# A two-layer hybrid trunk in split fp32: gate and up products as one 512-wide and one 256-wide matmul instead of three 256-wide

## The chip, the cores and the metric

The kernel runs on one core of a Trainium2 chip. The metric is the device time of one execution in microseconds (us). Engines are named as in the profile: PE (TensorE; PEld is its weight load), DVE (VectorE), ACT (ScalarE), POOL (GpSimd), SP (SyncE, which issues the loads).

## What is computed

256 tokens of width 1024 pass through two layers. Each layer is a half-step SwiGLU feed-forward, a mixing part (sparse attention in 8 heads beside a gated linear recurrence in 4), and a second half-step feed-forward:

```python
def swiglu(x, w_gate, w_up, w_down):
    return (jax.nn.silu(x @ w_gate) * (x @ w_up)) @ w_down

for l in range(DEPTH):                                   # 2
    x = x + 0.5 * swiglu(rmsnorm(x, ffn1_norm[l]), ffn1_w_gate[l], ffn1_w_up[l], ffn1_w_down[l])
    h = rmsnorm(x, mix_norm[l])
    proj = h @ w_in[l]
    ...
    x = x + jnp.concatenate([o_nsa, o_hg], axis=-1) @ w_out[l]
    x = x + 0.5 * swiglu(rmsnorm(x, ffn2_norm[l]), ffn2_w_gate[l], ffn2_w_up[l], ffn2_w_down[l])
```

The gate and up weights are 1024 x 2816, the down weights 2816 x 1024, all in fp32. So there are four feed-forwards in a run.

## The kernel before

**Split products.** A product W x in fp32 is made of three matmuls in the type fp32r: W's high part with x's high part, W's high part with x's low part, and W's low part with x's high part. The names `hi` and `lo` are the parts of a unit of weights, `xh` and `xl` those of the normed activations (transposed: 128 rows of the width by 256 tokens, 8 such tiles), `th` and `tl` those of the hidden activations.

**The stream of weights.** Weights come in units of 512 KB (1024 columns by 128 partitions) through SP into one of three `raw` buffers. ACT copies a unit to `hi` (L313), DVE, in the mixing part POOL also, subtracts it to `lo` (L326, L328); five split units are held (`RING`). A unit's place comes free when the matmuls have used it.

**Two ways of multiplying.** In `stream` (L463 to L465) 128 tokens of one half h are the stationary operand and 512 columns of weights move; the result of half h goes to an accumulator of `acc0` for h = 0 and of `acc1` for h = 1. In `wide_unit` (L493 to L495) 128 columns of weights are the stationary operand and all 256 tokens move; a block of 256 columns is [128, 2, 256], one PSUM bank. `acc0` and `acc1` have two slots each, each slot a tile of its own of one bank.

**A feed-forward.** First a block of 256 gate and 256 up columns goes through `stream`, one for each half (`both_done` at its end; in the very first feed-forward it uses activations that still lack the norm's factor, `rs`). Then ten times a gate block through `wide_unit` in `acc0` and an up block in `acc1`, each of two units with 2 x 4 steps (c, t). When a gate block ends, ACT reads it with Silu into a buffer `sg`; when an up block ends, DVE multiplies it by that `sg`; ACT copies the result to `th`, DVE subtracts to `tl`. Then the down product goes through `stream`, two blocks of 512 columns for each half, and DVE adds each to the residual (`resid`, L653). The mixing part's w_in and w_out products go through `stream` too, except the 512 columns each of `hf` and `hq` of the recurrence, which go through `wide_unit`.

**The order.** The order of instructions is not written down but made by a planner while the program is built: `Sched.run` holds generators as tasks, and at each step emits the op that could start first by modelled costs, plus a penalty by kind of task. An op with several engines to choose from (a copy, a subtraction) goes to the one that would end it first. Each engine then runs its instructions in that order, and waits for others by semaphores, which the tile framework sets from who wrote and read which tile.

Of the kernel before, what the change touches and what calls it, by code (L numbers as in the profile page):

```python
# [25 lines left out]
LARGE = 85.0   # the exponential of more could overflow  # L26
LEVELS = [0, 1, 2, 4, 8, 16, 32]

# columns of the constant array
# [9 lines left out]
# moving layout of the keys of a group: sel 1 | sel 0 | win 0 | win 1 | compressed  # L39
# [5 lines left out]
RING = 5       # split weight units held  # L45
RAW = 3        # unsplit weight units held
BOOT = 3       # units split by K tiles at the start
# when the rest of the inputs is loaded: after which unit of weights, half, from and to which 256 columns
BOOT_X = ((-1, 0, 1, 2), (0, 0, 2, 4), (2, 1, 0, 2), (3, 1, 2, 4))
FIRST = (-0.3, -0.4, 0.5, 1.3, 0.1, 0.6, 0.9, 0.2)  # L50
LAG = 4        # units by which the halves of the tokens are apart at a phase's ends
NBUF = 14      # general buffers of the mixing part
# [3 lines left out]
# how eager the tasks are (less: earlier)  # L56
# [43 lines left out]
class Op:  # L100
    """An instruction (or a few for one engine), with the engines that could run it, each with what it costs there."""
# [15 lines left out]
LOAD = 1.28    # a switch of ScalarE's tables  # L117
# [4 lines left out]
class Sched:  # L122
    """Emits the instructions of tasks that run side by side, in the order in which they could start.

    A task is a generator. It yields an Op (and is sent the op's end), or a request: wait for a key
    or a condition, set a key, acquire a slot (sent the slot), release it. An op waits for what its
    task has waited for or done before."""
# [26 lines left out]
    def resolve(self, t):  # L154
        """A request that isn't an op; whether it could be met."""
# [37 lines left out]
    def run(self):  # L193
        while self.tasks:
# [29 lines left out]
            if eng == "DMA":  # L224
                # its issue, then the transfer, which others hold up
                issued = end - cost + 0.475
                self.moved = max(issued + 0.65, self.moved) + cost
                end = self.moved + 0.87
# [7 lines left out]
def four(t):  # L236
    """Two K tiles of 512 columns as four of 256."""
    return t.rearrange("p a (b n) -> p (a b) n", b=2)
# [29 lines left out]
class Block:  # L268
    """Columns of a product that share an accumulator: [128 tokens, n] for each half, or, where the weights are the
    stationary operand, [128 columns, 2, 256 tokens]."""  # L270

    def __init__(self, n, done, wide=None):
        self.n, self.done, self.wide, self.ps = n, done, wide, {}


class Unit:
    """1024 x 128 of a block's weights: two K tiles of 512 columns, or four of 256."""
# [6 lines left out]
class Trunk(Sched):  # L284
    def __init__(self, ctx, tc, io, out):
# [5 lines left out]
        bank = lambda n: psum.tile([128, 512], F32, name=n)  # L291
        for h in range(2):
            self.slots[f"acc{h}"] = [(bank(f"acc{h}{i}"), []) for i in range(2)]
# [24 lines left out]
    def copy(self, out, in_, after=None):  # L318
        """A copy, by either of two engines."""
# [36 lines left out]
    def transposes(self, pairs):  # L356
        """pairs: (out, in)."""
# [9 lines left out]
    def rope_norm(self, st, n):  # L367
        """st [128, 2, n]: sums of squares in, inverse norms out, both in the first row."""
        yield self.ts(st[:, 1], st[:, 0], 1.0 / n[1], EPS, op0=OP.mult, op1=OP.add)
        yield self.rsqrt(st[:, 0], st[:, 1])  # L370

# [107 lines left out]
    def wide_unit(self, i, u, p):  # L479
# [4 lines left out]
        if u.first:  # L484
            (k.ps[0],) = yield acq(f"acc{k.wide}")
        ps = k.ps[0].rearrange("p (c t) -> p c t", c=2)
        hi, lo = (four(x) for x in self.split_w[i])
        f = self.nc.tensor.matmul

# [7 lines left out]
        def two(c, t):  # L497
            mm(c, t)
            mm(c, t + 1)

        for c in range(2):
            for t in (0, 2):
                yield self.P(6 * (0.0025 + 256 / 2400), lambda: two(c, t))
# [21 lines left out]
    def control(self):  # L525
        """One phase's memory after the other's."""
# [8 lines left out]
    def start(self):  # L535
        nc, per = self.nc, self.per
        self.X, self.XN, self.ss, self.rs = [], [], [], []
        self.XH, self.XL = (per.tile([128, 8, 256], F32R, name=n) for n in ("xh", "xl"))
# [22 lines left out]
    def pad(self):  # L561
        """Zeros that stay, of what only in part takes data."""
# [10 lines left out]
    def boot(self):  # L573
        """What the start waits for, in the order in which it is needed."""
# [34 lines left out]
    def first_turn(self, h, n):  # L609
        """The first product starts before the norm is known: of the inputs times the gains, transposed."""  # L610
# [47 lines left out]
    def norm(self, h, i):  # L658
        """The i-th norm of the half h: its transposed, split activations."""
# [32 lines left out]
    def ffn(self, l, pre):  # L692
# [27 lines left out]

        def wide_gate_done(b):
            def done(ps):
                yield wait(("open", p))
                (sg,) = yield acq("sg")
                yield self.A(sg, ps, AF.Silu)
                yield rel("acc0", ps)
# [4 lines left out]
        def wide_up_done(b):  # L731
            def done(ps):
                yield wait(("wg", p, b))
                sg = st["wg", b]
                yield self.tt(sg, ps, sg, OP.mult)
                yield rel("acc1", ps)
# [12 lines left out]
        for c in range(10):  # L749
            for a, (w, d) in enumerate(((wg, wide_gate_done), (wu, wide_up_done))):  # L750
                b = Block(512, d(c), wide=a)
# [27 lines left out]
        def opened(pool, p):  # L779
            self.slots["sg"] = [(pool.tile([128, 512], F32, name=f"sg{i}"), []) for i in range(4)]  # L780
# [58 lines left out]
    def mix(self, l):  # L839
# [69 lines left out]
        def values(h, br, src):  # L909
            """src [128, g, 64] -> split, between columns of zeros."""  # L910
# [171 lines left out]
        def attend_task(h, g):  # L1082
# [3 lines left out]
            # the heads' segments: branch, where in the scores, width, mask  # L1086
# [443 lines left out]
```

## Time and profile before

| | us |
|---|---|
| median of three runs | 1146.16 |
| the runs | 1146.1, 1149.26, 1146.16 |
| span of the profiled execution | 1147.0 |
| PE busy in it | 1080.8 (94%) |
| DVE busy | 720.7 (63%) |
| ACT busy | 571.7 (50%) |
| POOL busy | 200.5 (17%) |
| DMA, mean | 162 GB/s |

The profile is of one execution, and its span is 0.84 us above the median. The durations below are from it. An engine that is idle waits for what stands behind the arrow in its row. In rows of PE the time from one start to the next says what a matmul costs in a stream; the duration printed includes its passage through the array and overlaps the next one.

### The profile page before, as it was taken

How to read it: one execution, taken by the hardware profiler on the slowest of the kernel's cores; microseconds unless marked ns; L12 is line 12 of the kernel's file. 1: busy time of each engine (PE TensorE's matmuls, PEld its weight loads, DVE VectorE, ACT ScalarE, POOL GpSimd, SP SyncE). 2: the span in 40 equal slices, each digit the busy share in tenths (PEclk: the TensorE clock that was granted, in tenths of full speed). 3: DMA queues.
4: the chain of work that ended last, by engine and by line, in shares of the span. 5: the costliest groups of instructions: out<-in, count | busy, mean ns of one | idle time of the engine just before them, and what ended most of it. 6: DMA issues, size and time to landing. Idle time of an engine off the chain costs nothing.

```text
span 1147.0 us, 18786 instructions
## 1 busy us (share of the span) xinstructions
PE 1080.8 (94%) x7420; PEld 974.6 (85%) x7420; DVE 720.7 (63%) x1187; ACT 571.7 (50%) x899; POOL 200.5 (17%) x193
## 2 busy tenths in 40 slices
PE   5999999988879999999999999999898799999998
PEld 4999988777668799998879999877876688999986
DVE  5565544777998665554465555447889976655543
ACT  5554444465756554444354444434675555444432
POOL 2200000353554200000020000013635622000000
PEclk9999999998989999999999999999998899999999
DMA  7666655564313476666666666555551235766553
GB/s 220 197 188 194 188 185 185 148 167 129 110 55 93 147 200 187 184 185 184 188 171 199 187 178 190 181 161 160 144 167 56 74 110 145 204 184 183 183 157 121
DMA packets 154168, 186.16 MB, mean 162 GB/s; under 512 B 7568, under 2 KB 117984, under 8 KB 154080
## 3 DMA queue, kind: packets, MB, share of 16 engines
q1 hardware_dynamic: 154080, 184.96, 54.7%
q8 instruction: 58, 0.95, 0.3%
q14 instruction: 30, 0.25, 0.1%
HBM read 183.89 MB, written 1.05 MB: 161 GB/s over the span
## 4 chain that ended last, share of the span: by engine, by line
PE 75%; DVE 16%; issue 4%; DMA 2%; ACT 1%; POOL 1%; SPq 1%; DVEq 0%; POOLq 0%; ACTq 0%
PE acc L493 14%; PE acc L494 14%; PE acc L495 14%; PE acc L463 9%; PE acc L465 9%; PE acc L464 9%; DVE buf L326 2%; PE short L360 2%; DVE lo L326 2%; DVE xn L668 1%; DVE buf L1156 1%; DVE hx L326 1%; DVE kk L336 1%; DVE P L326 1%; DVE ptl L326 1%
## 5 line engine op out<-in xcount | busy, mean ns | idle before, releaser
L326 DVE TENSOR_TENSOR lo<-raw,hi 128x1024 fp32r<-128x1024 f32 (+2 forms) x302 | 365.6, 1214 | 286.5 <-ACT hi L313 285.5
L313 ACT ACTIVATE hi<-raw 128x1024 fp32r<-128x1024 f32 (+2 forms) x337 | 350.6, 1043 | 309.2 <-PE acc L465 110.8
L493 PE MATMUL acc<-xh,hi 128*128 128x256 f32 x1408 | 402.4, 286 | 0.0
L494 PE MATMUL acc<-xl,hi 128*128 128x256 f32 x1408 | 401.1, 285 | 0.0
L495 PE MATMUL acc<-xh,lo 128*128 128x256 f32 x1408 | 400.9, 285 | 0.0
L493 PEld LDWEIGHTS acc<-xh,hi 128*128 128x128 f32 x1408 | 273.2, 194 | 0.2
L494 PEld LDWEIGHTS acc<-xl,hi 128*128 128x128 f32 x1408 | 273.1, 194 | 0.1
L495 PEld LDWEIGHTS acc<-xh,lo 128*128 128x128 f32 x1408 | 273.0, 194 | 0.0
L463 PE MATMUL acc<-hi,th 128*128 128x512 f32 x352 | 139.5, 396 | 0.0
L464 PE MATMUL acc<-lo,th 128*128 128x512 f32 x352 | 139.2, 395 | 0.0
L465 PE MATMUL acc<-hi,tl 128*128 128x512 f32 x352 | 139.1, 395 | 0.0
L354 POOL TENSOR_TENSOR rs<-rs,half 128x1 f32<-128x1 f32 x12 | 7.0, 587 | 552.2 <-DVE rs L661 552.2
L328 POOL TENSOR_TENSOR lo<-raw,hi 128x1024 fp32r<-128x1024 f32 (+1 forms) x37 | 89.4, 2422 | 68.6 <-ACT hi L313 43.2
L463 PE MATMUL acc<-hi,xh 128*128 128x512 f32 (+1 forms) x240 | 98.6, 411 | 0.0
L465 PE MATMUL acc<-hi,xl 128*128 128x512 f32 (+1 forms) x240 | 93.0, 387 | 0.0
L464 PE MATMUL acc<-lo,xh 128*128 128x512 f32 (+1 forms) x240 | 92.7, 386 | 0.0
L465 PEld LDWEIGHTS acc<-hi,tl 128*128 128x128 f32 x352 | 66.1, 188 | 16.1
L463 PEld LDWEIGHTS acc<-hi,th 128*128 128x128 f32 x352 | 66.2, 188 | 15.6
L464 PEld LDWEIGHTS acc<-lo,th 128*128 128x128 f32 x352 | 66.1, 188 | 15.6
L313 ACT ACTIVATE sg<-acc 128x512 f32<-128x512 f32 (+1 forms) x46 | 26.1, 568 | 66.8 <-PE acc L495 64.4
L465 PEld LDWEIGHTS acc<-hi,xl 128*128 128x128 f32 x240 | 46.2, 193 | 9.3
L463 PEld LDWEIGHTS acc<-hi,xh 128*128 128x128 f32 x240 | 46.8, 195 | 6.8
(233 smaller groups left out, 1174.9 us busy)
## 6 DMA issues: line engine op xcount, KB each, us to landing
raw<-in_ffn_w_down_dram SPq DMA_DIRECT2D x88, 512.0 KB, 4.0
raw<-in_ffn_w_gate_dram SPq DMA_DIRECT2D x80, 512.0 KB, 3.8
raw<-in_ffn_w_up_dram SPq DMA_DIRECT2D x80, 512.0 KB, 4.1
raw<-in_w_in_dram SPq DMA_DIRECT2D x48, 512.0 KB, 3.7
raw<-in_w_out_dram SPq DMA_DIRECT2D x16, 512.0 KB, 3.8
buf<-in_cmp_w_dram SPq DMA_DIRECT2D x16, 256.0 KB, 5.1
raw<-in_ffn_w_gate_dram SPq DMA_DIRECT2D x13, 256.0 KB, 2.8
raw<-in_ffn_w_up_dram SPq DMA_DIRECT2D x13, 256.0 KB, 3.1
```

The source lines that it names most:

```text
L313: return ("ACT", c, lambda: self.nc.scalar.activation(out, in_, func, **k), TABLES.get(func))
L326: alts = [("DVE", 0.065 + 0.00104 * n, lambda: self.nc.vector.tensor_tensor(out, a, b, op), None)]
L328: alts.append(("POOL", 0.13 + 0.00213 * n, lambda: self.nc.gpsimd.tensor_tensor(out, a, b, op), None))
L336: lambda: self.nc.vector.tensor_scalar(out, a, s1, s2, **k), None)]
L360: self.nc.tensor.transpose(o, i, self.ident[:i.shape[0], :i.shape[0]])
L463: f(ps[:, :k.n], ah, hi[:, t, :k.n], start=st, stop=False)
L464: f(ps[:, :k.n], ah, lo[:, t, :k.n], start=False, stop=False)
L465: f(ps[:, :k.n], al, hi[:, t, :k.n], start=False, stop=sp)
L493: f(ps[:, c], hi[:, t, j], xh, start=u.first and c == t == 0, stop=False)
L494: f(ps[:, c], hi[:, t, j], xl, start=False, stop=False)
L495: f(ps[:, c], lo[:, t, j], xh, start=False, stop=u.last and c == 1 and t == 3)
L668: toks.append((yield self.V(576, lambda: nc.vector.scalar_tensor_tensor(self.XN[h][:, c], self.X[h][:, c], rs[:, 0:1], self.gains[0][:, c] ...
```

## The change

The two slots of `acc0` become the two halves (one bank each) of one tile `pair[0]` of [128, 2, 512], and so those of `acc1` in `pair[1]`. `xh` and `xl` become the halves of one tile `xx`, so that for each of the 8 K tiles the 256 columns of the high part and the 256 of the low part lie side by side. A gate or up block is now "paired": it takes both slots of its accumulator. A step (c, t) is one 512-wide matmul of the weights' high part with both parts of the activations (L500, into bank c), and one 256-wide of the weights' low part with the high part (L501, into the first half of the same bank). At a block's end `both_parts` adds the two halves: ACT copies the second halves of the two banks into an `sg` buffer, DVE adds the first halves. A gate block's Silu then runs from `sg` to `sg`; an up block takes an `sg` buffer of its own, for which there are now five, and the multiply reads two of them. The planner's cost of a group of steps changes with the number of matmuls. `hf` and `hq` keep three matmuls. Comments and docstrings, which the new file has not, are left out here.

```diff
-    def __init__(self, n, done, wide=None):
-        self.n, self.done, self.wide, self.ps = n, done, wide, {}
+    def __init__(self, n, done, wide=None, paired=False):
+        self.n, self.done, self.wide, self.paired, self.ps = n, done, wide, paired, {}
...
         bank = lambda n: psum.tile([128, 512], F32, name=n)
+        self.pair = []
         for h in range(2):
-            self.slots[f"acc{h}"] = [(bank(f"acc{h}{i}"), []) for i in range(2)]
+            t = psum.tile([128, 2, 512], F32, name=f"acc{h}")
+            self.pair.append(t)
+            self.slots[f"acc{h}"] = [(t[:, i], []) for i in range(2)]
         self.slots["short"] = [(bank(f"short{i}"), []) for i in range(3)]
         self.slots["po"] = [(bank("po"), [])]
         big = lambda n, dt: self.per.tile([128, 2, 512], dt, name=n)
...
             yield wait(u.need(h))
         k = u.block
         if u.first:
-            (k.ps[0],) = yield acq(f"acc{k.wide}")
-        ps = k.ps[0].rearrange("p (c t) -> p c t", c=2)
+            if k.paired:
+                k.ps[0] = yield acq(f"acc{k.wide}", 2)
+            else:
+                (k.ps[0],) = yield acq(f"acc{k.wide}")
+        ps = k.ps[0] if k.paired else k.ps[0].rearrange("p (c t) -> p c t", c=2)
         hi, lo = (four(x) for x in self.split_w[i])
         f = self.nc.tensor.matmul
+        def mm2(c, t):
+            j = slice(128 * c, 128 * c + 128)
+            x = self.XX[:, u.kt + t].rearrange("p a t -> p (a t)")
+            f(self.pair[k.wide][:, c], hi[:, t, j], x, start=u.first and t == 0, stop=False)
+            f(self.pair[k.wide][:, c, :256], lo[:, t, j], x[:, :256], start=False, stop=u.last and t == 3)
 
         def mm(c, t):
             j = slice(128 * c, 128 * c + 128)
...
             f(ps[:, c], lo[:, t, j], xh, start=False, stop=u.last and c == 1 and t == 3)
 
         def two(c, t):
-            mm(c, t)
-            mm(c, t + 1)
+            for x in (t, t + 1):
+                mm2(c, x) if k.paired else mm(c, x)
 
         for c in range(2):
             for t in (0, 2):
-                yield self.P(6 * (0.0025 + 256 / 2400), lambda: two(c, t))
+                yield self.P((4 if k.paired else 6) * 0.0133 + 0.64, lambda: two(c, t))
         yield rel("ring", self.split_w.pop(i))
         yield put(("wide", i))
         if u.last:
...
-        self.XH, self.XL = (per.tile([128, 8, 256], F32R, name=n) for n in ("xh", "xl"))
+        self.XX = per.tile([128, 8, 2, 256], F32R, name="xx")
+        self.XH, self.XL = self.XX[:, :, 0], self.XX[:, :, 1]
...
 
+        def both_parts(x, a):
+            x, t = x.rearrange("p (c t) -> p c t", c=2), self.pair[a]
+            yield self.A(x, t[:, :, 256:])
+            yield self.tt(x, t[:, :, :256], x, OP.add)
         def wide_gate_done(b):
             def done(ps):
                 yield wait(("open", p))
                 (sg,) = yield acq("sg")
-                yield self.A(sg, ps, AF.Silu)
-                yield rel("acc0", ps)
+                yield from both_parts(sg, 0)
+                yield rel("acc0", *ps)
+                yield self.A(sg, sg, AF.Silu)
                 st["wg", b] = sg
                 yield put(("wg", p, b))
             return done
 
         def wide_up_done(b):
             def done(ps):
+                (up,) = yield acq("sg")
+                yield from both_parts(up, 1)
+                yield rel("acc1", *ps)
                 yield wait(("wg", p, b))
                 sg = st["wg", b]
-                yield self.tt(sg, ps, sg, OP.mult)
-                yield rel("acc1", ps)
+                yield self.tt(sg, up, sg, OP.mult)
+                yield rel("sg", up)
                 s = slice(2 + 2 * b, 4 + 2 * b)
                 yield from self.split(st["th"][:, s], st["tl"][:, s], sg.rearrange("p (c t) -> p c t", c=2))
                 yield rel("sg", sg)
...
-                b = Block(512, d(c), wide=a)
+                b = Block(512, d(c), wide=a, paired=True)
...
-            self.slots["sg"] = [(pool.tile([128, 512], F32, name=f"sg{i}"), []) for i in range(4)]
+            self.slots["sg"] = [(pool.tile([128, 512], F32, name=f"sg{i}"), []) for i in range(5)]
```

The number of matmuls falls from 7420 by 1280. In the rows that follow, a name's number tells buffers apart: before, `acc00_63` and `acc01_64` are the two banks of `acc0`, `acc10_65` and `acc11_66` those of `acc1`; now `acc0_63` and `acc1_64` are the two tiles of two banks.

PE at the start of the first gate block of the first feed-forward. Before:

```order
L360 MATMUL short1_68<-ident_94,xn1_91 128x128 [waits DVE_49]
L360 MATMUL short1_68<-ident_94,xn1_91 128x128 x3
L493 MATMUL acc01_64<-xh_84,hi4_82 128x256 [waits Activation_49]
L494 MATMUL acc01_64<-xl_85,hi4_82 128x256 [waits DVE_49]
L495 MATMUL acc01_64<-xh_84,lo4_83 128x256
```

Now:

```order
L364 MATMUL short1_66<-ident_91,xn1_88 128x128 [waits DVE_49]
L364 MATMUL short1_66<-ident_91,xn1_88 128x128 x3
L364 MATMUL short0_65<-ident_91,sg0_121 128x128 [waits DVE_49]
L364 MATMUL short0_65<-ident_91,sg0_121 128x128
L364 MATMUL short2_67<-ident_91,sg1_122 128x128 [waits DVE_49]
L364 MATMUL short2_67<-ident_91,sg1_122 128x128
L500 MATMUL acc0_63<-xx_82,hi4_80 128x512 [waits Activation_49]
L501 MATMUL acc0_63<-xx_82,lo4_81 128x256
```

Before, the gate block starts in the second bank of `acc0`, and the transposes of `sg0` and `sg1` (the first block's result) come 36 rows later; now they stand ahead of the gate block's first matmul.

DVE in the middle of gate and up, from the end of one block. Before it is the multiply at the end of an up block, then the units of the next, then the multiply of the next:

```order
L326 TENSOR_TENSOR sg2_126<-acc11_66,sg2_126 128x512 [waits PE_49]
L326 TENSOR_TENSOR lo3_81<-raw1_72,hi3_80 128x1024 [waits DMAHW7_49,Activation_49]
L326 TENSOR_TENSOR tl_129<-sg2_126,th_128 128x512 [waits Activation_49]
L326 TENSOR_TENSOR lo4_83<-raw2_73,hi4_82 128x1024 [waits DMAHW0_49,PE_49,Activation_49]
L326 TENSOR_TENSOR lo0_75<-raw0_71,hi0_74 128x1024 [waits DMAHW1_49,PE_49,Activation_49]
L326 TENSOR_TENSOR lo1_77<-raw1_72,hi1_76 128x1024 [waits DMAHW2_49,PE_49,Activation_49]
L326 TENSOR_TENSOR sg3_127<-acc10_65,sg3_127 128x512 [waits PE_49]
```

Now it starts with the add at the end of a gate block:

```order
L330 TENSOR_TENSOR sg2_123<-acc0_63,sg2_123 128x512 [waits Activation_49]
L330 TENSOR_TENSOR lo2_77<-raw1_70,hi2_76 128x1024 [waits DMAHW1_49,Activation_49]
L330 TENSOR_TENSOR lo3_79<-raw2_71,hi3_78 128x1024 [waits DMAHW2_49,PE_49,Activation_49]
L330 TENSOR_TENSOR sg0_121<-acc1_64,sg0_121 128x512 [waits Activation_49]
L330 TENSOR_TENSOR sg2_123<-sg0_121,sg2_123 128x512 [waits DVE_49]
L330 TENSOR_TENSOR lo4_81<-raw0_69,hi4_80 128x1024 [waits DMAHW3_49,Activation_49]
L330 TENSOR_TENSOR tl_127<-sg2_123,th_126 128x512 [waits Activation_49]
L330 TENSOR_TENSOR lo0_73<-raw1_70,hi0_72 128x1024 [waits DMAHW4_49,PE_49,Activation_49]
L330 TENSOR_TENSOR sg4_125<-acc0_63,sg4_125 128x512 [waits Activation_49]
```

The read of `acc0` at a gate block's end has moved from ACT's Silu to a copy by ACT and this add, and that of `acc1` likewise; the multiply now reads two `sg` buffers.

DVE where the mixing part scales the queries of the second half, just behind the w_in block of q in `acc1`. Before:

```order
L336 TENSOR_SCALAR qst1_1936<-qst1_1936 128x8
L326 TENSOR_TENSOR lo0_75<-raw0_71,hi0_74 128x2x280 [waits DMAHW7_49,Activation_49]
L326 TENSOR_TENSOR buf4_1891<-acc11_66,qst1_1936 128x512 [waits Pool_49]
L326 TENSOR_TENSOR buf3_1890<-buf4_1891,cg_116 128x512 [waits DVE_49]
L326 TENSOR_TENSOR buf5_1892<-buf4_1891,sgn_117 128x8x32 x2
```

Now:

```order
L340 TENSOR_SCALAR qst1_1654<-qst1_1654 128x8
L330 TENSOR_TENSOR lo0_73<-raw0_69,hi0_72 128x2x280 [waits DMAHW7_49,Activation_49]
L330 TENSOR_TENSOR buf4_1609<-acc1_64,qst1_1654 128x512 [waits PE_49,Pool_49]
L330 TENSOR_TENSOR buf3_1608<-buf4_1609,cg_113 128x512 [waits DVE_49]
L330 TENSOR_TENSOR buf5_1610<-buf4_1609,sgn_114 128x8x32 x2
```

The read of `acc1` now also waits for PE: matmuls of the next w_in block have been written into the other bank of `acc1` ahead of it, and those that follow on PE wait for this read. Before, the read waited for POOL alone, and the next block went on in the other bank.

## Rows read from the trace of the kernel before

**Rows 1.** The page: busy time by engine; the chain that ended last, by engine.

```profile
PE 1080.8 (94%) x7420; PEld 974.6 (85%) x7420; DVE 720.7 (63%) x1187; ACT 571.7 (50%) x899; POOL 200.5 (17%) x193
...
PE 75%; DVE 16%; issue 4%; DMA 2%; ACT 1%; POOL 1%; SPq 1%; DVEq 0%; POOLq 0%; ACTq 0%
```

**Rows 2.** Busy time by stretch: from:to, length, PE, PEld, DVE, ACT, POOL, PEclk, DMA.

```profile
80.00:120.00 40.00, 40.00 (x336) 40.00 (x335) 23.26 (x23) 18.37 (x21) 0.00 (x0) 1.00 0.69 197
...
240.00:280.00 40.00, 32.53 (x236) 32.16 (x236) 32.18 (x59) 24.92 (x43) 20.36 (x18) 0.87 0.46 128
...
320.00:360.00 40.00, 33.91 (x303) 29.22 (x304) 37.53 (x98) 25.10 (x58) 22.93 (x20) 0.87 0.27 80
```

**Rows 3.** Groups, 80 to 120 us: busy us, mean ns, idle before, releasers.

```profile
L326 DVE TENSOR_TENSOR lo<-raw,hi 128x1024 fp32r<-128x1024 f32 x15 | 18.4, 1225 | 15.5 <-ACT hi L313 15.5
L313 ACT ACTIVATE hi<-raw 128x1024 fp32r<-128x1024 f32 x14 | 14.8, 1058 | 15.7 <-PE acc L494 10.6 <-issue 2.6 <-DVE sg L326 1.9
L326 DVE TENSOR_TENSOR sg<-acc,sg 128x512 f32<-128x512 f32 x4 | 2.8, 689 | 1.9 <-PE acc L495 1.9
...
L313 ACT ACTIVATE th<-sg 128x512 fp32r<-128x512 f32 x4 | 2.5, 614 | 0.0
L313 ACT ACTIVATE sg<-acc 128x512 f32<-128x512 f32 x3 | 1.8, 597 | 4.9 <-PE acc L495 4.9
```

**Rows 4.** Rows of PE in gate and up: start us, duration us, line, operation.

```profile
100.06 0.28 PE L494 MATMUL acc<-xl,hi 128*128 128x256 f32 x1
...
100.30 0.28 PE L493 MATMUL acc<-xh,hi 128*128 128x256 f32 x1
```

**Rows 5.** Rows of PE in w_in, in order of time.

```profile
234.73 0.39 PE L463 MATMUL acc<-hi,xh 128*128 128x512 f32 x1
...
235.41 0.39 PE L463 MATMUL acc<-hi,xh 128*128 128x512 f32 x1
```

**Rows 6.** Rows of PE in the down product.

```profile
170.01 0.40 PE L465 MATMUL acc<-hi,tl 128*128 128x512 f32 x1
...
170.71 0.40 PE L465 MATMUL acc<-hi,tl 128*128 128x512 f32 x1
```

**Rows 7.** Rows of PE, ACT and DVE at the first FFN's start.

```profile
32.83 0.36 PE L493 MATMUL acc<-xh,hi 128*128 128x256 f32 x1
...
35.97 0.84 ACT L313 ACTIVATE sg<-acc,rs 128x256 f32<-128x256 f32 x2
...
36.48 0.87 DVE L708 SCALAR_TENSOR_TENSOR sg<-acc,rs,sg 128x256 f32<-128x256 f32 x2 [0.56 <-ACT sg L313]
...
37.10 0.28 PE L495 MATMUL acc<-xh,lo 128*128 128x256 f32 x1
...
37.22 0.62 PE L360 MATMUL short<-ident,sg 128*128 128x128 f32 x4
```

**Rows 8.** A row of DVE at the turn of down.

```profile
178.85 0.69 DVE L653 SCALAR_TENSOR_TENSOR x<-acc,x 128x512 f32<-128x512 f32 x1 [1.88 <-PE acc L465]
```

**Rows 9.** PE and ACT in the first mixing stage [idle before <-releaser].

```profile
231.22 0.50 PE L898 MATMUL short<-identr,pth 128*128 128x128 f32 x4 [1.39 <-DVE pth L326]
...
231.76 0.60 ACT L313 ACTIVATE qs<-short 128x512 fp32r<-128x512 f32 x1 [0.35 <-PE short L898]
...
238.08 0.36 ACT L313 ACTIVATE buf<-acc 128x256 f32<-128x256 f32 x1
...
238.38 0.53 PE L898 MATMUL short<-identr,pth 128*128 128x128 f32 x4 [0.77 <-DVE pth L326]
...
257.78 1.11 PE L360 MATMUL short<-ident,buf 128*128 128x128 f32 x4 [2.98 <-DVE buf L322]
...
272.11 0.87 PE L360 MATMUL short<-ident,buf 128*128 128x128 f32 x3 [4.48 <-DVE buf L322]
```

**Rows 10.** Groups on POOL and DVE, 220 to 400 us, one operation.

```profile
L328 POOL TENSOR_TENSOR S<-S,P 128x256 f32<-128x256 f32 x6 | 5.8, 968 | 1.6 <-DVE P L326 1.6
...
L326 DVE TENSOR_TENSOR S<-S,P 128x256 f32<-128x256 f32 x8 | 4.2, 522 | 0.0
```

## The prediction

> **What bounds the kernel now.** I read the page first, then stretches, then groups of instructions inside a stretch, then the order of rows on one engine. The page says that PE is busy for 1080.8 of 1147.0 us, and the chain of waits that ended last runs through PE for 75% and through DVE for 16% [rows 1]. That is a mean over two kinds of stage. In a gate and up stage (80 to 120 us) PE is busy 40.00 of 40 us at a granted clock of 1.00, that is 2.4 GHz, while DVE has 23.26 and ACT 18.37; in the first layer's mixing stage PE is busy only 32.5 to 33.9 of 40, the clock falls to 0.87, and DVE has 32.2 to 37.5 [rows 2]. So in gate and up every nanosecond between two matmuls counts, and in the mixing stage what counts is the chain from PE to ACT or DVE and back. That PE sets the pace in gate and up is also seen from the other side: ACT's copies to `hi` sat idle 15.7 us of these 40, mostly until a matmul gave its ring place back [rows 3].
>
> **The pairs.** A gate or up block takes two units of 8 (c, t) steps; four FFNs x 10 x 2 blocks x 2 units x 8 give 1280 steps. Each was three 256-wide matmuls and becomes one 512-wide and one 256-wide. Two of the 256-wide take 100.06 to 100.30, start to start: 120 ns each, 360 ns a step [rows 4]. Two rows could price the 512-wide. In w_in three take 234.73 to 235.41, 0.680 us, 226.7 ns each [rows 5]; in the down product three take 170.01 to 170.71, 0.700 us, 233.3 ns each [rows 6]. A step then costs 346.7 or 353.3 ns, so it gains 13.3 or 6.7 ns, in sum 17.0 or 8.5 us. I take 17.0: at 2.4 GHz 256 columns are 106.7 ns and 512 are 213.3, so the 120 of today and the 226.7 of w_in have the same fixed part, 13.3 ns, and the new matmul reads the same `xh`, `xl` values and uses the same weights tiles as these. I know no reason for the longer fixed part of the down product, so its 8.5 stays as a bound. Two matmuls of one fixed part less could not give more than 13.3 ns a step unless the remaining 256-wide got quicker, for which no row speaks.
>
> The Trainium skill (TensorE: Matmul & The Clock Gate, Back-to-back issue gap) gives an isolated gap of N / 2.4 + 2.5 ns. This trace does not agree with it: 256 columns would be 109.2 against the 120 of the rows, and 512 would be 215.8 against 226.7. By that rule a step would go from 327.5 to 325.0 ns and the whole change would be worth 3.2 us instead of 17.0, so it speaks against the change; the measurement decides here.
>
> **What a block's end costs now.** Per gate block ACT gets a copy of 128x512 from PSUM in place of the Silu from PSUM (597 ns), then a Silu from SBUF; I price the latter by `th<-sg`, the same size from SBUF, 614 ns. DVE gets an add of 128x512 (689 ns, as its multiply from PSUM), and per up block ACT one more copy and DVE one more multiply [rows 3]. Per gate and up pair that is on ACT 4 x 1.058 (`hi`) + 2 x 0.597 (copies) + 2 x 0.614 (Silu, `th`) = 6.65 us and on DVE 4 x 1.225 (`lo`) + 4 x 0.689 (add twice, multiply and `tl`, all of one size) = 7.66 us, against 32 x 0.347 = 11.1 us of PE. Both fit, with 3.4 us left on DVE: nothing. A wait is added too: the gate block of the next c writes both banks of `acc0`, so its first matmul waits for DVE's add of the gate block before. Between them lies a whole up block, 16 x 0.347 = 5.55 us, and copy and add take 0.60 + 0.69, with at most one `hi` (1.06) and one `lo` (1.23) queued ahead on their engines, 3.6 us. What is queued behind that matmul on PE is everything, but `lo` runs up to five units ahead. I take 0; if the cover were gone, each of 72 waits (9 in each accumulator of four FFNs) would cost the excess.
>
> **The start of the first FFN.** Before, the first gate block began at 32.83 in the second bank of `acc0`, while the first bank still held the first FFN's first block; it ran 37 matmuls until 37.10, and the transposes of `sg` followed at 37.22. ACT's Silu of that first block starts only at 35.97 and DVE's product at 36.48 [rows 7]. Now the gate block needs both banks, so the four transposes stand ahead of it, and PE idles from 32.83 to where they could run: 37.22 - 32.83 = 4.4 us, once. Weights that arrive meanwhile can't give it back, since PE then sets the pace. In the other FFNs that first block needs no such late scale, and the up block in `acc1` comes 5.5 us later: 0.
>
> **One tile of two banks.** `acc0` and `acc1` are now one tile each, and a write into one bank waits for a read of the other: the order shows waits that no row of before had. They cost three things. (1) From down's first to its second 512 columns: six matmuls (1.4 us) of the other half lie between the last matmul and the next write, and DVE's residual takes 0.69 [rows 8] and can have a `lo` of 1.22 ahead: 0 to 0.75 each, eight of them, 0 to 6 us; I take 0.2 each, 1.6, since most of DVE's time there is idle. (2) In the mixing stages I find eleven places per layer where the next write follows the read with nothing or one step between: q 2, keys and values 3, hf 1, hq and hi 3, the out product 2. A read by ACT takes 0.36 us, by DVE 0.69 (as the residual's); with the drain of the last matmul (0.39 long at a pitch of 0.23) and two hand-overs of 0.04 (the transposes at 231.22 end at 231.72, ACT's read of them starts at 231.76) that is 0.6 to 0.93 us each [rows 5, 8, 9], so 6.6 to 10.2 a layer, 8.4 in the middle. Against that PE already waits there for the same chains: 1.39, 0.77, 2.98 and 4.48 us in the first layer, 9.6 in sum [rows 9]. Where a wait falls ahead of such an old one, it disappears in it, unless it delays the chain that the old one waited for. About half do: the q and key reads feed that chain itself. So 0 to 20.4 for both layers, and I take half of the middle, 4.2 a layer, 8.4. (3) The order moves about a dozen small tensor ops per mixing layer from POOL to DVE, some 8 us of DVE's time where it has 2.5 to 8 us of 40 free [rows 2]. The same op takes 968 ns on POOL and 522 on DVE [rows 10], so each is over sooner and others start later: -8 to +8 a layer, and I take 0.
>
> **The sum** is made against the profiled 1147.0: -17.0 + 4.4 + 1.6 + 8.4 = -2.6, 1144.4. The median of the runs shown, 1146.16, is 0.84 below the span, so **1143.6**.
>
> **The rivals.**
> - The mixing waits are all absorbed in the old ones (for: 9.6 us of PE waits a layer against 8.4 of new ones; against: the q reads feed the chain that the old ones wait for). Then 8.4 less: 1135.2. Chance 0.25.
> - The 512-wide runs at the down product's pace (for: it is the other stage in which 512 columns run for long at clock 1.00; against: other operands). 8.5 more: 1152.1. Chance 0.14.
> - Slower by serialisation: in the mixing stages a read of one bank of an accumulator shuts out writes to its other bank, and every one of the eleven waits lies on the chain from DVE to PE. At 10.2 a layer instead of 4.2 the time is 1155.6; it turns slower than before once the eleven cost over 5.5 us a layer, 0.5 each, net. For: DVE has 37.5 of 40 us between 320 and 360. Chance 0.18.
> - The pair doesn't do what it says: a 512-wide takes what two 256-wide take, 240 ns, and there is no part of a matmul that two in one save (for: the 233.3 of the down product is half way there; against: the 226.7 of w_in). No gain: 1160.6. Chance 0.05. The rule of the Trainium skill named above gives nearly this, 1157.4; the 120 ns of the rows speaks against it.
> - More gain than I see, with the waits absorbed, under 1131: 0.03.
>
> The forecast itself has 0.35.
>
> **How the numbers follow.** A measurement of this kernel can tell some 0.3%, 3.4 us, from no change, so same is 1142.7 to 1149.6. The absorbed case, the last one and a third of the forecast's give faster 0.40; the rest of the forecast and a little of the pace case give same 0.26; slower is 0.34. The range runs from 1131 (a bit below the absorbed case, with down at 0 and a little less at the start) to 1157 (serialisation with its down waits), which leaves the no-gain case and the tail below out.
>
> **What would show it.** In the after trace, the start to start of a pair in gate and up (0.347 or 0.353), with PE busy 40 of 40 there; one PE idle of 4 to 5 us near 33; DVE's `resid` as releaser of PE at the turn of down; ACT and DVE reads of `acc` as releasers of PE in the mixing stages, and the length of these stages, which I expect 4 us longer each. The forecast is wrong if a gate block's first matmul waits for DVE's add each time, or if mixing stages lengthen by far more or less than 4 us.

## The result, and the profile after

The changed kernel takes 1196.97 us (median; 1195.47 to 1199.95), the kernel before 1146.63 beside it: a ratio of 1.0439, 95% interval 1.0413 to 1.0464. It is 50 us slower, where 1143.6 was forecast and 1157 was the end of the range. The page of its profiled execution, busy time and share by engine, and in forty slices of the span the granted clock and the share of the DMA engines:

```profile
span 1193.7 us, 16456 instructions
...
PE 1104.4 (93%) x6140; PEld 918.3 (77%) x6140; DVE 785.0 (66%) x1289; ACT 618.8 (52%) x979; POOL 177.5 (15%) x169
...
PEclk9899999999787899999999999999989698999999
DMA  7566655454250266666666666555435004766654
```

Against [rows 1] there are 1280 matmuls fewer, and PE is still busy longer: 1104.4 us against 1080.8. A busy share hides a slow clock, and the slices of PEclk show where to look: its lowest digits, two 7 and a 6, stand in the two mixing stages, and beside one 7 and the 6 the DMA engines stand at 0. To see what each stage does I took the start of the first matmul of each stage from the rows of PE, in both traces. The time from one start to the next:

| stage | before | after | difference |
|---|---|---|---|
| to the first gate block (from the span's start) | 32.83 | 36.09 | +3.3 |
| gate and up, four times | 116.42, 115.39, 116.38, 115.39 | 115.73, 113.26, 111.62, 113.26 | -9.7 |
| down, the first three | 63.71, 63.72, 63.71 | 63.70, 63.71, 63.72 | 0.0 |
| down, the last, to its last matmul | 61.36 | 62.33 | +1.0 |
| first block of the third feed-forward | 12.57 | 12.61 | 0.0 |
| w_in up to `hf`, twice | 33.05, 33.12 | 34.82, 34.86 | +3.5 |
| `hf` and `hq`, twice | 35.52, 33.99 | 36.41, 34.59 | +1.5 |
| `hi` to the next gate block, twice | 121.74, 123.87 | 146.82, 145.93 | +47.1 |

One line holds the loss. It is the stretch from the first `hi` matmul over attention, recurrence and w_out to the next feed-forward, in both layers alike. By stretches of 40 us (from:to, length, busy time of PE, PEld, DVE, ACT, POOL, granted clock, DMA share, GB/s):

```profile
240.00:280.00 40.00, 31.76 (x235) 29.98 (x234) 31.43 (x59) 21.89 (x41) 19.68 (x14) 0.96 0.49 137
280.00:320.00 40.00, 31.38 (x279) 23.25 (x279) 34.81 (x56) 22.20 (x41) 22.56 (x21) 0.87 0.33 98
320.00:360.00 40.00, 31.76 (x218) 23.99 (x219) 31.43 (x133) 23.60 (x69) 8.71 (x11) 0.79 0.43 119
360.00:400.00 40.00, 36.43 (x211) 31.39 (x212) 24.21 (x94) 18.38 (x51) 2.08 (x6) 0.83 0.03 7
400.00:440.00 40.00, 36.66 (x168) 29.43 (x168) 25.27 (x31) 21.31 (x32) 11.98 (x7) 0.91 0.49 145
```

The same numbers for the whole stretch from `hi` to the next gate block in the first layer, before and after:

```profile
281.53:403.27 121.74, 108.64 (x808) 89.47 (x807) 102.86 (x289) 76.81 (x179) 54.33 (x51) 0.94 0.36 107
...
286.75:433.57 146.82, 124.62 (x808) 97.26 (x807) 106.96 (x298) 77.19 (x180) 43.75 (x40) 0.85 0.30 86
```

The stretch is 25.1 us longer. DVE has 4.1 us more to do in it, ACT 0.4, and POOL 10.6 less; PE runs the same 808 matmuls, at a lower clock. So the stage is not longer because an engine has more to do. From 360 to 400 the weights stop (7 GB/s): the split units that are held are those of w_out, and w_out waits for attention. SP's queue issues no load of weights between these two:

```profile
341.97 1.05 SPq L354 DMA_DIRECT2D raw<-in_w_out_dram  x1
397.90 0.37 SPq L354 DMA_DIRECT2D raw<-in_ffn_w_gate_dram  x1
```

What came late is seen in the rows of PE and of SP's queue. After, the first `hi` matmul, the transposes of the keys, and the loads of the compression's weights that follow them:

```profile
286.75 0.39 PE L467 MATMUL acc<-hi,xx 128*128 128x512 f32 x1
...
335.37 1.03 PE L364 MATMUL short<-ident,buf 128*128 128x128 f32 x8
...
335.99 5.88 SPq L354 DMA_DIRECT2D buf<-in_cmp_w_dram  x8
```

And the same rows before:

```profile
281.53 0.40 PE L463 MATMUL acc<-hi,xh 128*128 128x512 f32 x1
...
282.94 1.03 PE L360 MATMUL short<-ident,buf 128*128 128x128 f32 x8
...
283.57 5.72 SPq L350 DMA_DIRECT2D buf<-in_cmp_w_dram  x8
```

Before, they stand 1.4 us behind the first `hi` matmul (281.53), and attention runs side by side with the recurrence. After, they stand 48.6 us behind it (286.75), when nearly all products of the recurrence are done (those on `hx` end at 330.5), and attention runs nearly alone. Nothing makes PE wait there. The keys of the second half were ready 65 us earlier, with this copy:

```profile
269.74 0.29 DVE L326 COPY buf<-buf 128x256 f32<-128x256 f32 x1
```

The planner emitted the task `k_turn`, which holds these transposes, that late, and engines run in the order in which they were given their work. `k_turn` has a penalty of 0.15, and so has the stream of weights in its plain case (`FLOW[1]`); the planner takes the op with the least start plus penalty, and of equal ones the task that stands first in its list, which is the stream.

### The profile page after: what moved, and what is told of

Read it like the earlier page. It is cut to its first block, busy times and chain, and to the rows that moved or that the text cites. A ratio compares the mean times of both kernels' runs of the same rounds, so it can differ in the third digit from the quotient of the medians.

```text
span 1193.7 us, 16456 instructions
## 1 busy us (share of the span) xinstructions
PE 1104.4 (93%) x6140; PEld 918.3 (77%) x6140; DVE 785.0 (66%) x1289; ACT 618.8 (52%) x979; POOL 177.5 (15%) x169
## 4 chain that ended last, share of the span: by engine, by line
PE 73%; DVE 16%; issue 5%; ACT 3%; DMA 1%; SPq 1%; POOL 0%; DVEq 0%; ACTq 0%; POOLq 0%
PE acc L500 25%; PE acc L501 13%; PE acc L467 10%; PE acc L469 10%; PE acc L468 10%; DVE buf L330 3%; DVE lo L330 2%; PE short L364 2%; DVE P L330 1%; DVE xn L682 1%; DVE buf L1180 1%; ACT buf L317 1%; DVE hx L330 1%; PE short L1370 1%; ACT hi L317 1%
## 5 line engine op out<-in xcount | busy, mean ns | idle before, releaser
L500 PE MATMUL acc<-xx,hi 128*128 128x512 f32 x1280 | 452.8, 399 | 0.0
L501 PE MATMUL acc<-xx,lo 128*128 128x256 f32 x1280 | 359.0, 281 | 0.0
L500 PEld LDWEIGHTS acc<-xx,hi 128*128 128x128 f32 x1280 | 241.4, 189 | 59.0
L501 PEld LDWEIGHTS acc<-xx,lo 128*128 128x128 f32 x1280 | 242.4, 189 | 0.1
L317 ACT ACTIVATE sg<-acc 128x512 f32<-128x512 f32 (+1 forms) x86 | 50.2, 583 | 133.5 <-PE acc L501 131.1
L330 DVE TENSOR_TENSOR sg<-acc,sg 128x512 f32<-128x512 f32 (+1 forms) x86 | 57.9, 673 | 86.7 <-ACT sg L317 86.7
L467 PE MATMUL acc<-hi,xx 128*128 128x512 f32 (+1 forms) x240 | 103.6, 432 | 10.6 <-DVE x L667 5.1
L468 PE MATMUL acc<-lo,xx 128*128 128x512 f32 (+1 forms) x240 | 95.4, 398 | 0.6 <-DVE lo L330 0.6
L469 PE MATMUL acc<-hi,xx 128*128 128x512 f32 (+1 forms) x240 | 95.2, 397 | 0.0
L467 PEld LDWEIGHTS acc<-hi,xx 128*128 128x128 f32 x240 | 47.7, 199 | 22.5 <-DVE x L667 6.0
L469 PEld LDWEIGHTS acc<-hi,xx 128*128 128x128 f32 x240 | 47.8, 199 | 9.9
L468 PEld LDWEIGHTS acc<-lo,xx 128*128 128x128 f32 x240 | 48.2, 201 | 7.5 <-DVE lo L330 1.3
```

Of the source, the lines that this page charges most:

```text
L317: return ("ACT", c, lambda: self.nc.scalar.activation(out, in_, func, **k), TABLES.get(func))
L330: alts = [("DVE", 0.065 + 0.00104 * n, lambda: self.nc.vector.tensor_tensor(out, a, b, op), None)]
L467: f(ps[:, :k.n], ah, hi[:, t, :k.n], start=st, stop=False)
L468: f(ps[:, :k.n], ah, lo[:, t, :k.n], start=False, stop=False)
L469: f(ps[:, :k.n], al, hi[:, t, :k.n], start=False, stop=sp)
L500: f(self.pair[k.wide][:, c], hi[:, t, j], x, start=u.first and t == 0, stop=False)
```

## The experiments

Two theories were set against each other. ORDER: the loss comes from the planner's late emission of the key transposes. BANKS: it comes from the waits between the two banks of an accumulator that are now one tile, the mechanism of the slower rival. BANKS has an edit that touches it alone: in e2 PE's order stays that of the change, row by row. ORDER has one number of the planner's table (e1, e4), and the planner then plans anew all that follows.

**The key transposes early again (e1), in the changed kernel.**

```diff
-       "last_product": -0.15, "k_turn": 0.15, ...
+       "last_product": -0.15, "k_turn": 0.1, ...
```

> The changed kernel with one number of the planner's table altered: the penalty of the task that transposes the keys (k_turn) goes from 0.15 to 0.10, so that it is emitted ahead of the stream of w_in again. In the changed kernel the planner emits it some 43 us later than in the kernel before, behind the whole of the recurrence's products. Theory ORDER (the 47 us come from that one delay): the stretch from the first hi matmul to the next gate block falls from 146.8 and 145.9 us back to 122 to 125 in both layers, and the time to 1149 to 1153. Theory BANKS (they come from the waits between the two banks of one accumulator tile): the time stays within 5 us of 1197.

Measured: 1163.94 us (1162.48 to 1165.2), ratio to the kernel before 1.0139 (1.0118 to 1.0159), 33 us faster than the change. The transposes now stand ahead of `hi` (296.13), earlier than they stood before, in two groups with those of the compression's input. The second group:

```profile
268.36 1.07 PE L364 MATMUL short<-ident,buf 128*128 128x128 f32 x8 [1.04 <-DVE buf L326]
```

The stretch from `hi` to the next gate block falls to 118.94 and 117.80, below before; but that from `hf` to `hi` grows to 48.47 and 48.73, so the two together are 167.4 and 166.5 against 183.2 and 180.5 after, and 157.3 and 157.9 before. Most of the loss hung on one number of the planner's table. It is not all, and the 1149 to 1153 of ORDER was too low: the shared banks are still there (e2), and the planner's order with 0.10 is not that of before.

**Four tiles of one bank, in the changed kernel, same order (e2).** The pair becomes two tiles; copy and add at a block's end go bank by bank.

```diff
-            t = psum.tile([128, 2, 512], F32, name=f"acc{h}")
+            t = [bank(f"acc{h}{i}") for i in range(2)]
...
-            yield self.A(x, t[:, :, 256:])
-            yield self.tt(x, t[:, :, :256], x, OP.add)
+            def halves():
+                for c in range(2):
+                    nc.scalar.activation(x[:, c], t[c][:, 256:], AF.Copy)
+            def adds():
+                for c in range(2):
+                    nc.vector.tensor_tensor(x[:, c], t[c][:, :256], x[:, c], OP.add)
+            yield Op(("ACT", 0.052 + 0.000833 * 512, halves, TABLES.get(AF.Copy)))
+            yield Op(("DVE", 0.065 + 0.00104 * 512, adds, None))
```

> The changed kernel with the order of instructions as it is, but each accumulator bank a tile of its own again (the copy and the add at a block's end go as two of 128x256 each). Theory ORDER: only the w_in stretches give back what they grew by, 1.8 + 0.9 and 1.7 + 0.6 us, so about 1192 (1189 to 1195). Theory BANKS: the mixing stages fall back, 1148 to 1155.

Measured: 1181.68 (1175.43 to 1183.52), ratio 1.0284 (1.0249 to 1.0319), 15.3 us faster than the change. More than ORDER said, far less than BANKS said. The w_in stretches are back at 33.04 and 33.07, `hf` and `hq` give 5.6 and 2.3 us, the last stretch stays at 146.38 and 142.58. So the shared tile costs some 15 us, and not the 47. Each stretch is read from one execution: `hf` and `hq` take 32.9 to 35.7 us in those runs below and before that have the order of before and a tile for each bank, so differences of under 3 us there mean little.

**Both edits (e3),** that is the two diffs above together.

> Both edits, the early key transposes and the four bank tiles: what the 512-wide matmul alone is worth in an order like that of before. Theory ORDER: 1143 to 1149, that is the kernel before less the 9.7 us that gate and up stages gained, plus 3.3 at the start of the first feed-forward, plus or minus what the planner's other moves cost. Theory BANKS: as the run with four banks, 1148 to 1155.

Measured: 1151.99 (1148.71 to 1155.84), ratio 1.0034 (1.0019 to 1.005): 45 us faster than the change, where the two edits alone gave 33 and 15. They nearly add up. The time misses the 1143 to 1149 of ORDER and lies in the range that BANKS gave here; by e1 and e2 BANKS is out all the same. Against before it is still 0.3% slower, with `hf` to the next gate block at 162.9 and 162.1.

**The kernel before, key transposes late (e4).** Here nothing of the change is in the kernel.

```diff
-       "last_product": -0.15, "k_turn": 0.15, ...
+       "last_product": -0.15, "k_turn": 0.3, ...
```

> The kernel before, with the penalty of the key transposes raised from 0.15 to 0.30 and nothing else: the planner now emits them 30 us later in the first layer and 51 us later in the second. Theory ORDER: the stretch from hi to the next gate block grows by 15 to 25 us in the first layer and by 20 to 30 in the second, and the time is 1180 to 1200. Theory BANKS: 1147 within 4 us, since no bank is shared.

Measured: 1188.61 (1185.86 to 1191.07), ratio 1.0353 (1.0328 to 1.0378). The transposes move to

```profile
329.77 1.03 PE L360 MATMUL short<-ident,buf 128*128 128x128 f32 x8
```

and the trace takes the look of the changed kernel, with the same stop of the weights:

```profile
320.00:360.00 40.00, 30.77 (x196) 22.78 (x195) 32.60 (x160) 27.77 (x91) 6.69 (x14) 0.76 0.39 106
360.00:400.00 40.00, 36.78 (x224) 32.67 (x224) 21.91 (x60) 15.95 (x31) 6.07 (x6) 0.89 0.05 14
```

`hi` to the next gate block takes 143.98 and 143.90. The time lies in ORDER's range and far from BANKS's. Raising the penalty of `k_turn` alone costs 40 us, without a paired block and without a shared bank. But one number is not one move: the planner plans what follows anew, and POOL has 177 instructions in place of 193. The recorded order with only the key transposes moved was not run, so how much of the 40 is their place alone, and how much what moved with them, is not shown.

**The old order with the new matmuls (f1, f2, f3), and before with shared banks (f4).** To take the order out of the comparison, the order of the kernel before was recorded, and the planner made to follow it: of the ops that are ready it takes the one that stood first there, on the engine that it had there. The copy, add and Silu (or multiply) of a block's end take the place of the one op that they replace.

```diff
-                pen = t.pen() if callable(t.pen) else t.pen
+                spot, fixed = place(t)
...
-                        one = (done, start + pen + more, eng, start + cost, cost, fn, tab)
+                        one = (done, spot, eng, start + cost, cost, fn, tab)
```

f1 has four bank tiles, f2 the tile of two banks as in the change. f3 is f1 with the very first gate block unpaired, in one bank. f4 is the kernel before with the two banks of each accumulator in one tile, and nothing else. Here `place` is a task's place in the recorded order; the edits of f3 (the unpaired block ends with the Silu of before, left out here) and f4 are

```diff
 f3
-                b = Block(512, d(c), wide=a, paired=True)
+                paired = not first or c > 0 or a == 1
+                b = Block(512, d(c) if a else d(c, paired), wide=a, paired=paired)
 f4
-            self.slots[f"acc{h}"] = [(bank(f"acc{h}{i}"), []) for i in range(2)]
+            t = psum.tile([128, 2, 512], F32, name=f"acc{h}")
+            self.slots[f"acc{h}"] = [(t[:, i], []) for i in range(2)]
```

> The 512-wide matmul alone: the changed kernel with four bank tiles, and with the planner made to follow the recorded order of the kernel before (each instruction at its old place and on its old engine; the new copy, add and Silu of a block's end at the place of the old Silu or multiply). The mixing stages should then be those of before (157 us from hf to the next gate block in both layers). Theory ORDER: gate and up stages give back 9 to 10 us, the pause at the first gate block costs 4.4 and the cold matmuls behind it 2: 1140 to 1145, against 1147. If pairing costs something of its own elsewhere: over 1148.

> The same as the last run, but with the two banks of an accumulator as one tile, as in the change: what the waits between the banks cost in the old order. In the change's order they cost 15.3 us. Theory ORDER: 12 to 20 us more than the last run, 1153 to 1165. A theory that they cost only where the order is bad: within 4 us of the last run.

> As the first run of this call (old order, four bank tiles), but the very first gate block keeps three 256-wide matmuls and one bank, so that it need not wait for the first block's end. Theory ORDER: the pause of 4.4 us near 33 and the slow matmuls behind it go: 1134 to 1139, faster than both kernels. If the pause was hidden: as the first run.

> The kernel before with one edit: the two banks of each accumulator are one tile; no pairing, same order. Theory ORDER: 12 to 20 us slower, 1158 to 1168, in the w_in and mixing stages and at the turn of the down product. A theory that they cost only where the order is bad: 1147 to 1151.

| run | us (lowest to highest) | ratio to before (interval) |
|---|---|---|
| f1, paired, old order | 1142.21 (1140.7 to 1143.36) | 0.9945 (0.9929 to 0.9961) |
| f2, the same, shared banks | 1157.26 (1152.74 to 1159.69) | 1.0074 (1.0052 to 1.0097) |
| f3, f1 with the first gate block unpaired | 1138.98 (1136.96 to 1140.09) | 0.9918 (0.9904 to 0.9931) |
| f4, before with shared banks | 1162.81 (1160.88 to 1164.07) | 1.0126 (1.0111 to 1.0141) |

f1 and f2 came as theory ORDER said, f3 at the upper end and f4 in its range. The shared tile costs 15.1 us in the paired kernel of old order (f2 against f1), 15.1 in the kernel before (f4), 15.3 in the change's own order (e2): it is a cost by itself, with either order. Which reads hold PE up is seen in f2, in its waits of PE from 216 to 410 us (engine, line, releaser: us in total, times, longest):

```profile
PE acc L571 <- ACT buf L421: 1.1, 2, 0.7
PE acc L571 <- DVE x L771: 0.9, 1, 0.9
PE acc L571 <- DVE buf L434: 0.9, 1, 0.9
```

They are four waits, the longest 0.9 us, each with matmuls into the other bank behind it, and f1 has none of these lines. They sum to 2.9 us; from f1 to f2 the first mixing stage grows by 4.6. From f2 to the change as it was made, that is from the old order to the planner's own, the time goes from 1157.26 to 1196.97: the order as a whole costs 40 us.

**The price of a 512-wide matmul (g1), and of grouping (g2).** Both on f3; in g2 `part` 0 is the 512-wide matmul of a step and 1 the 256-wide, so that two of one size follow each other.

```diff
 g1
-            f(self.pair[k.wide][c][:, :256], lo[:, t, j], x[:, :256], start=False, stop=u.last and t == 3)
+            f(self.pair[k.wide][c], lo[:, t, j], x, start=False, stop=u.last and t == 3)
 g2
-            for x in (t, t + 1):
-                mm2(c, x) if k.paired else mm(c, x)
+            if k.paired:
+                for part in range(2):
+                    mm2(c, t, part)
+                    mm2(c, t + 1, part)
```

> What a 512-wide matmul costs in gate and up by itself: the version with the old order, four banks and the old first gate block, in which the weights' low part too meets both parts of the activations, so that a step is two 512-wide matmuls (the product of the two low parts is added to the sum). Theory FIXED PART (a matmul is 0.4167 ns a column and 13.3 ns): 0.453 us a step. Theory COLUMNS (the price goes by columns, 0.469 ns each as in the 256-wide of before): 0.480 us a step. The rows of the changed kernel show 231 to 241 ns, so 0.462 to 0.482 are open; a gate and up stage of 320 steps takes 145 us by the first and 154 us by the second.

> The version with the old order, four banks and the old first gate block, with two steps grouped: two 512-wide matmuls, then two 256-wide, in place of one and one in turn. In the changed kernel a step takes 0.354 us in three feed-forwards and 0.347 in one, each in a fixed pattern of three steps. Theory PATTERN (which pattern the queue falls into depends on the alternation): the stages that took 113.3 us change, by up to 2.3 us down or 2 up, and the run is 1134 to 1142. Theory SIZE (the sum of sizes alone counts): within 0.5 us of 113.3 for each stage, and 1139.

g1 is one run, 1268.16; what counts is its rows, here in the second feed-forward:

```profile
450.03 0.39 PE L604 MATMUL acc<-xx,hi 128*128 128x512 f32 x1
...
450.94 0.39 PE L604 MATMUL acc<-xx,hi 128*128 128x512 f32 x1
```

Four 512-wide in 0.91 us, 227 each, as in [rows 5]; the stages take 145.00 to 146.46 us, the 145 of FIXED PART. Alone in a gate and up stage a 512-wide has the price that was forecast. In turn with a 256-wide it has not. Rows of the changed kernel in the first feed-forward, where three steps go from 103.77 to 104.83, 0.353 us each, and in the third, where three go from 630.07 to 631.11, 0.347 each:

```profile
103.77 0.40 PE L500 MATMUL acc<-xx,hi 128*128 128x512 f32 x1
104.00 0.28 PE L501 MATMUL acc<-xx,lo 128*128 128x256 f32 x1
104.12 0.40 PE L500 MATMUL acc<-xx,hi 128*128 128x512 f32 x1
...
104.83 0.40 PE L500 MATMUL acc<-xx,hi 128*128 128x512 f32 x1
```

```profile
630.07 0.39 PE L500 MATMUL acc<-xx,hi 128*128 128x512 f32 x1
...
631.11 0.40 PE L500 MATMUL acc<-xx,hi 128*128 128x512 f32 x1
```

The same instructions on the same tiles keep one pattern of three steps (361, 349 and 350 ns) through most of a feed-forward, or another (343 to 350). What decides between them is not shown. Grouped by two (g2) the second and fourth gate and up stages go from 113.28 to 111.69, the first stays near 112.8 and the third near 112.5, and the run is 1135.44 (1132.92 to 1137.75), ratio 0.9877 (0.9852 to 0.9902). PATTERN holds against SIZE: two stages changed by 1.6 us where SIZE allowed 0.5. g2 is faster than both kernels, 1.2% below before.

## Why the prediction was wrong, point by point

- **What moved (the third point of the shared tile)** is the step that failed: a dozen small ops moved from POOL to DVE, "-8 to +8 a layer, and I take 0". I read the new order by counting, for each engine and stage, what was added and removed. A count shows which engine an op went to and not where it stands, and the key transposes stand in both orders once, on the same engine. By f2 against the change the new order costs 40 us, and by e4 a late `k_turn`, with what the planner then moves, costs 40 as well. The engine moves that the term did look at are small beside it: 4.1 us of DVE's time in a stretch that grew by 25.1. No rival held this case either, so the range ended 40 us too early.
- **The waits between banks.** Forecast 8.4 for mixing and 1.6 for the turns of down, with 0 and 20.4 as bounds. From f1 to f2 the stages of mixing grow by 10.8 us and those of down by 2.6, and the whole by 15.1. Mechanism right, size some 5 us short. f2, the change without its new order, stands at 1157.26 where the slower rival was put at 1155.6, but that is luck: the rival had 20.4 us for the mixing waits and too much gain for the pairs.
- **The pairs.** Forecast 13.3 ns a step. The second, third and fourth feed-forward gained 2.1, 4.8 and 2.1 us, 9.4 ns a step over 960 steps. The lone price of 227 was right (g1); that a 512-wide keeps it beside a 256-wide was assumed, and holds in no stage: the 512-wide take 231 to 241. The forecast sum of 347 a step comes out in one of four stages, there as 231 to 233 and 112 to 118, so the 256-wide did get quicker, for which the prediction saw no row. The other three show 353.9 a step or more, the sum of the rival with the down product's pace. 231 to 236, about the 233.3 of the row left as a bound, is what most rows of 512 columns in the trace before show: a count, and not a choice between two rows, would have told.
- **The start.** Forecast 4.4 us, one pause; measured 3.94 of idle, and what was missed stands behind it:

```profile
35.33 1.11 PE L364 MATMUL short<-ident,sg 128*128 128x128 f32 x4 [3.94 <-DVE sg L722]
36.09 0.78 PE L500 MATMUL acc<-xx,hi 128*128 128x512 f32 x1
...
36.88 0.63 PE L500 MATMUL acc<-xx,hi 128*128 128x512 f32 x1
...
37.52 0.63 PE L500 MATMUL acc<-xx,hi 128*128 128x512 f32 x1
```

  The steps behind the pause take 0.64 us, not 0.35, at a granted clock of 0.50 from 36 to 40 us:

```profile
36.00:38.00 2.00, 2.00 (x9) 1.71 (x8) 1.53 (x3) 0.82 (x3) 0.00 (x0) 0.50 1.02 323
38.00:40.00 2.00, 2.00 (x8) 1.71 (x7) 0.67 (x3) 0.00 (x0) 0.00 (x0) 0.50 0.69 246
```

  0.50 is 1.2 GHz. Six steps at 0.64 cost 1.7 us more than at 0.35, which is why the first feed-forward gained only 0.7. In [rows 7] PE ran through this place and stayed at 120 ns a matmul. In f1 the slow stretch after the pause is longer, to 42:

```profile
40.00:42.00 2.00, 2.00 (x8) 1.71 (x8) 0.00 (x0) 0.00 (x0) 0.00 (x0) 0.50 0.12 41
```

  In f3, with no pause, the stage up to the first gate block is 4.0 us shorter than in f1 and the gate and up stage behind it 3.6. The whole run is only 3.2 us shorter: in f3's trace `hf` and `hq` of the first layer take 2.8 us more and the third gate and up stage 1.4 more. So of the 7.6 us in these two stages the run got back less than half; why is not shown.
- **A block's end.** Forecast 0, and right: no matmul of a gate or up block is among those that wait for the add, and the down stages keep their 63.7 us.
- **The rivals.** "The pair doesn't do what it says" had 240 ns and no fixed part; g1's 227 against 120 for 256 columns denies it. The Trainium skill (TensorE: Matmul & The Clock Gate, Back-to-back issue gap) gives 215.8 for 512 columns as the gap of an isolated matmul. None of these streams agrees with it: 227 alone, 231 to 241 in turn.

The parts, from the runs: -5.5 for the pairs and the start (f1), +15.1 for the shared banks (f2), +40 for the order, 49.6 in sum, against the 50.3 measured. The three are steps on one way from the kernel before to the change, so their sum has to close and proves nothing; what speaks for the parts is that 15 comes out in e2 and f4 as well, and 40 in e4. Still open is why the planner, given paired blocks, no longer let the key transposes in: that the tie of 0.15 with the stream decides is read from its code and agrees with e1, but which edit of its input (two slots at once, other costs, more ops at a block's end) tipped it was not tried.

## What to carry to other kernels

Where a greedy planner sets the order, a local edit can move work two stages on; look up, in the new order, where the first instruction of each long chain stands, not only how many instructions each engine got. Run the edit also with the old order pinned, so that what it is worth and what its new order costs come apart: here the pairs, with a tile for each bank, were 0.5% faster (1.2% with the first block unpaired and the matmuls grouped), the shared tile made the kernel before 1.3% slower (f4), and the planner's new order cost 40 us, 3.4%. And two PSUM banks that are read and written at different times should be two tiles, even where one instruction would like to read both.

## What the runs showed of the hardware that I had not expected

- In gate and up a stream of equal matmuls has one price (120 ns for 256 columns before, 227 for 512 in g1), while the down product's 512-wide, also a stream of equals, take 231 to 236. Alternating sizes settle into a repeating pattern: 0.347 or 0.353 us for the same pair of instructions, kept for most of a stage of over 100 us. Two and two, the pair took 0.348 to 0.349 in all four stages.
- One idle of 3.94 us on PE was followed by a stretch at a granted clock of 0.50, to 40 us in the changed kernel and to 42 in f1. In f1 idle and slow steps together lengthened the first two stages by 7.6 us against f3, about twice the idle; the whole run was 3.2 us longer.
